# Low parts of feed-forward weights by an accumulating DMA in a two-layer hybrid decoder step on one Trainium2 core

## The chip, the cores and the metric

The program runs on one core of a Trainium2 chip. The metric is the device time of one execution in microseconds; the figure for a kernel is the median of its runs. The core has five engines with a queue of instructions each: TensorE (PE in the profile; PEld are its weight loads), VectorE (DVE), ScalarE (ACT), GpSimd (POOL) and SyncE (SP). DMAs are issued from the queues of ScalarE, SyncE and GpSimd and are carried out by 16 DMA engines.

## The reference

One inference step of a decoder of two layers, model width 1024, for 544 tokens: one prompt of 512 tokens and 8 decode streams of 4. All data is fp32.

```python
def _layer(x, pos0, st, p):
    x = x + 0.5 * _swiglu(_rmsnorm(x, p['norm_ffn1']), p['ffn1_in'], p['ffn1_out'])
    u = _rmsnorm(x, p['norm_mix']) @ p['w_in']
    ...                      # SSD, RWKV-7, S5 and pooling mixers, 256 columns each
    x = x + y @ p['w_out']
    x = x + 0.5 * _swiglu(_rmsnorm(x, p['norm_ffn2']), p['ffn2_in'], p['ffn2_out'])
def _swiglu(x, w_in, w_out):
    gate, up = jnp.split(x @ w_in, 2, axis=-1)
    return (jax.nn.silu(gate) * up) @ w_out        # inner width 2816
```

So there are four feed-forward layers, two around the mixers of each layer, and a final norm. The outputs are the normed activations and the new states of the mixers.

## The kernel before

**Products.** The activations lie feature-major on the chip, 8 tiles x of 128 rows by 544 tokens. Each fp32 operand of a product is split into a rounded part and a rest, both of type float32r: weights into whi and wlo, activations into xh and xl (hidden activations into hh and hl). A 128x128 block of weights takes three products for each half of the tokens (mm3, lines 807 to 815): whi with xh (line 813), whi with xl (814) and wlo with xh (815), that is 6 matmuls of 272 columns.

**Weights.** They are streamed once, in the order of use, as chunks of 8 blocks (CH=8), 512 KB each. fetch (lines 791 to 794) issues one DMA per chunk on ScalarE's queue into wraw, a buffer of its own kind with two copies. block (lines 795 to 806) works on half a chunk at a time (CB=4, 128x512): ScalarE casts it into whi (line 802), and an engine s.lo subtracts whi from the raw weights into wlo (line 803). s.lo is VectorE, but GpSimd during a part of the mixers. The pool wp holds three buffers each of whi and wlo. A raw buffer is free for the next fetch but one when both casts and both subtractions of its chunk have read it.

**A feed-forward layer** (ffn, lines 860 to 899). inph(m) forms one hidden tile: 8 blocks of gate and 8 of up, so two chunks. VectorE scales the gate by 1/rms (gt, line 878), ScalarE applies Silu (879), GpSimd multiplies by 1/rms (s, 880), VectorE multiplies by the up product (s, 881), ScalarE casts hh (883), GpSimd subtracts hl (884). outph(G) then adds a group of hidden tiles into the 8 tiles of x (893). The groups have 8, 8 and 6 hidden tiles, so a tile of x takes 8, 8 and 6 blocks. In the last group the norm of the next stage is prepared tile by tile: ScalarE squares (849), GpSimd sums (852). The first feed-forward layer also carries the making of the S5 tables (s5_prep) between its tiles, mainly on VectorE.

**Order.** Dependencies, semaphores and the order of each engine's queue are set by the Tile framework when the program is built, by a plan of its own and by the buffers that are free; the order of the lines is only its starting point. In the trace casts stand three half chunks ahead of TensorE's use.

Of the kernel before, what the change touches and what calls it, by code (L numbers as in the profile page):

```python
"""One inference step of the hybrid decoder: activations feature-major on chip, weights streamed once."""
# [6 lines left out]
def build_consts():  # L8
    c={}
    I=np.arange  # L10
    p=I(128)
# [8 lines left out]
    c['mak']=(same&(r[:,None]<r[None,:])).astype(np.float32)            # rows s, cols t  # L20
    c['min']=(r[:,None]<=I(64)[None,:]).astype(np.float32)
    c['mnoff']=(same&(r[None,:]<r[:,None])&(r[None,:]//16!=r[:,None]//16)).astype(np.float32)  # rows t, cols s
# [39 lines left out]
def colz(a): # [n*128] -> [128,n]  # L62
    return np.asarray(a).reshape(-1,128).T
# [14 lines left out]
def pack_mat(i,l):  # L78
    """[128, 2048]: w2 (2x128, rows 0-63), a2 (2x128, rows 64-127), g2 (256), pool (2x128, block diagonal) | glu (2 x 512)"""
    m=np.zeros((128,2048),np.float32)  # L80
    m[:64,0:256]=i['rwkv_w2'][l]; m[64:,256:512]=i['rwkv_a2'][l]; m[:,512:768]=i['rwkv_g2'][l]
    pw=i['pool_w'][l]
    for t in range(2):
        for g in range(2): m[g*64:g*64+64,768+t*128+g*64:768+t*128+g*64+64]=pw[t*2+g]
    gw=i['s5_glu_w'][l]
    m[:,1024:1536]=gw[:128]; m[:,1536:2048]=gw[128:]
    return m
# [7 lines left out]
def pack_s5h(i,l):  # L95
    re=i['state_s5_re'][l].transpose(2,1,0); im=i['state_s5_im'][l].transpose(2,1,0)  # n,g,b
    return np.ascontiguousarray(np.stack([np.concatenate([re,im],0),np.concatenate([im,re],0)]))
def merge(*flows):
    """interleaves generators by the time that they yield: flows are (start, pace, generator)"""
    q=[[t,i,f,g] for i,(t,f,g) in enumerate(flows)]  # L100
    while q:
        e=min(q,key=lambda e:(e[0],e[1]))
        try: e[0]+=e[2]*next(e[3])
        except StopIteration: q.remove(e)
class Mix:
# [14 lines left out]
    def mm544(s,lhsT,rhs,fn):  # L120
        """fn(psum [128,272], column slice) for the two halves of lhsT^T @ rhs [128,544]"""
        for i in range(2):
            ps=s.bank()[:,:H]; c=slice(i*H,(i+1)*H)
            s.nc.tensor.matmul(ps,lhsT,rhs[:,c],start=True,stop=True)
            fn(ps,c)
    def rsqrt(s,new,ss):
        """-2/sqrt of an SBUF tile, with one Newton step"""
# [7 lines left out]
    def rwkv_prep(s,U,fp,tp,R):  # L135
        """U: name -> flat tile [128,553] (called when needed). Decay-scaled operands of the chunked recurrence, into R."""
# [61 lines left out]
    def masked(s,E,t,src):  # L198
        """t [128,n,2,64] = src [128,n,64] in column block h for the rows of head h, zero elsewhere"""
# [5 lines left out]
    def rwkv_inv(s,R,hf,tp,qp):  # L205
        """for 4 chunks of 64: block-diagonal A operands and the transposed inverses of I - tril(A B^T)"""
# [19 lines left out]
        # triangular inverses of the 16x16 diagonal blocks: one block per lane  # L226
# [17 lines left out]
        # T = T16 + R T, R = T16 N off the diagonal blocks, R^4 = 0; the last step gives T^T  # L244
# [25 lines left out]
    def rwkv_quarter(s,R,q,tp,qp):  # L270
        """token-major and masked operands of 2 chunks x 2 pairs of heads"""
# [26 lines left out]
    def rwkv_chain(s,R,q,qp):  # L298
        """two chunks of the recurrence; R['ST'] is the state [(h,j), pair, (h,i)]"""
# [106 lines left out]
    # ------------------------------------------------------------------ SSD  # L406
    def conv(s,u,j,out,t):
        """causal convolution of 4 taps and silu: u flat [128,576] to out [128,544]; t scratch [128,572]"""
# [5 lines left out]
    def ssd_dt(s,dtr,fp,SD):  # L414
        """dtr [4,544]; step sizes, decays and their sums, token-major [128, 4 chunks + sample, 4 heads]"""
# [13 lines left out]
        # softplus(x) = max(x,0) + log1p(exp(-|x|)), log1p(e) = 2 artanh(e/(2+e))  # L429
# [16 lines left out]
        # cumulative sums in the chunk, totals  # L446
# [18 lines left out]
    def ssd(s,R,xs,BB,CCt,z,H0,state_out,emit,tp):  # L465
        """xs 2 x [128,544]; BB, CCt [128,2,544]; z(t): silu of the gate [128,544]. H0 DRAM [128 n,8 b,4 h,64 p]"""
# [6 lines left out]
        for c in (4,0,1,2,3):  # L473
# [3 lines left out]
            # broadcast cumulative sums  # L477
# [11 lines left out]
            # token major x*dt and B  # L489
# [51 lines left out]
        # gate, norm  # L541
# [13 lines left out]
    # ------------------------------------------------------------------ pool  # L555
    def pool(s,U,emit,tp):
        """U(t): flat [128,684]: 15 rows before | 512 | 8 x (15 + 4)"""
# [23 lines left out]
    # ------------------------------------------------------------------ S5  # L581
    S5OFF=dict(TP=0,GT=2048,CO=4096,COS=6144,SS=7168,RHO=8192,A4=9216,B4=9232,END=9248)
    def s5_prep(s,par,name,tp):
        """par DRAM [128,1072]: lam_re, lam_im, log_step [16 each], b_re, b_im, c_re, c_im [256 each]; rows (re|im, n).
        Fills a DRAM scratch [128, END] with the matrices and tables of the chunked recurrence (8 tokens to a chunk)."""
# [12 lines left out]
        def sincos(E,y,sn,cs,k):  # L598
            """y is reduced in place to [-pi,pi]"""
# [22 lines left out]
        # (a - 1)/lam  # L622
# [11 lines left out]
        # A1 = (pr | pi), A2 = (pi | pr) by row half  # L634
# [11 lines left out]
        # phases of a^8 and the modulus  # L646
# [5 lines left out]
        for g0 in range(0,16,4):  # L652
# [3 lines left out]
            # C a^d, d = 0..8  # L656
# [3 lines left out]
            # a^(7-s) b: transposed to (s,c') rows  # L660
# [7 lines left out]
            # Toeplitz blocks: K[c',(d,c)] behind 128 zeros, row s takes the window that starts 16 s earlier  # L668
# [16 lines left out]
    def s5(s,U,prep,glu,H0,state_out,emit,fp):  # L685
        """U(t): [128,8,80] (position in the chunk, prompt chunks | 8 sample at 0..3 | 8 sample at 4..7); H0 DRAM [2,128,16,8] (state, halves swapped)"""
# [4 lines left out]
        ud=s.dram.tile([2,8,16,8,80],F32,name="ud",bufs=2)  # t, g, c', s, k  # L691
        yd=s.dram.tile([2,8,16,8,72],F32,name="yd",bufs=2)  # t, g, c, t, k
# [8 lines left out]
        for t in range(2):  # L701
# [28 lines left out]
            HP=tl("HP",[8,96])  # state before each chunk: 0, h_1 .. h_63 | 8 sample | pad ; h_64 apart  # L730
# [40 lines left out]
# the flows of the mixers: start and pace in the merged order of emission  # L771
FL=dict(s5=(0,1),prep=(0,1.25),rwkv=(0,1.1),back=(29,0.9),smp=(11,0.417),ssd=(2,0.8),rest=(66,1.373))
# column order of w_in: tiles (name, first column, width)
WIN=[('wa',1796),('k0',1284),('s0',2052),('r0',1028),('s1',2180),('v0',1540),('gd',1924),('k1',1412),('p0',2308),('p1',2436),('v1',1668),('r1',1156),('B1',640),('B0',512),('C0',768),('dt',1024),('C1',896),('x0',256),('x1',384),('z1',128),('z0',0)]
# rows of w_out by mixer tile: y = ssd 0-1, rwkv 2-3, s5 4-5, pool 6-7
# [3 lines left out]
class Kern(Mix):  # L779
    def __init__(s,tc,nc,ctx,io):  # L780
        Mix.__init__(s,tc,nc,ctx)
        s.io=io
        s.psd=s.P("psd",2,space=bass.MemoryType.PSUM)
        s.wp=s.P("wp",3); s.xhl=s.P("xhl",1); s.hole=ExitStack()
        s.wi=0; s.lo=nc.vector
# [9 lines left out]
    def block(s):  # L795
# [3 lines left out]
        if j==0:  # L799
# [3 lines left out]
            s.lo.tensor_tensor(lo,raw,hi.bitcast(F32),op=OP.subtract)  # L803
# [12 lines left out]
    def mmdt(s,ps,st,cols):  # L816
        """4 columns of the weights, twice in their block: rows 0-3 take the high part, rows 4-7 the low one"""
# [6 lines left out]
    def split(s,k,x,scale=None,pool=False):  # L824
        """x (times a per-partition scale) as two float32r tiles that sum to it"""
# [27 lines left out]
    def rstd(s,acc,tp,mp=None,tag=None):  # L853
        """-2/rms of the columns"""
# [5 lines left out]
    def ffn(s,st,gnext,bg=iter(())):  # L860
        nc=s.nc
        with s.tc.tile_pool(name="ffh",bufs=12,reuse_waits="tile") as hp, s.tc.tile_pool(name="fft",bufs=2,reuse_waits="tile") as tp, s.tc.tile_pool(name="ffr",bufs=1,reuse_waits="tile") as rp:
# [32 lines left out]
            for gi,G in enumerate(GROUPS):  # L895
                for m in (G if gi==0 else G[1:]): inph(m); m>1 and next(bg,None)
                if gi<2: inph(GROUPS[gi+1][0])
                outph(G,gi==2)
        return nst
    def tail(s,po,hs,acc,tp):  # L900
        """last tile of the last FFN and the final norm, one half of the tokens after the other"""
# [27 lines left out]
    def mixers(s,l,st):  # L929
        nc=s.nc; io=s.io; V=nc.vector; G=nc.gpsimd; A=nc.scalar  # L930
        # the residual waits in DRAM
# [156 lines left out]
    def do_prep(s):  # L1088
        """tables of the S5 recurrences, in pieces between the tiles of an FFN"""
# [84 lines left out]
```

## Time and profile before

| | us |
|---|---|
| median of 2 runs | 2331.2 |
| runs | 2331.07 to 2331.32 |
| span of the profiled execution, first to last instruction | 2330.7 |
| TensorE busy in that span | 2249.1 |

The page gives the profiled execution by its span alone; the runs above lie 0.4 to 0.6 us over that span. All rows below are of that one execution. Engines are named by PE, DVE, ACT, POOL and SP, a q behind the name means the engine's queue (a DMA issue), and Lnnn is the line of the kernel. What stands behind an arrow in brackets released the instruction after an idle time.

### The profile page before, as it was taken

How to read it: one execution, taken by the hardware profiler on the slowest of the kernel's cores; microseconds unless marked ns; L12 is line 12 of the kernel's file. 1: busy time of each engine (PE TensorE's matmuls, PEld its weight loads, DVE VectorE, ACT ScalarE, POOL GpSimd, SP SyncE). 2: the span in 40 equal slices, each digit the busy share in tenths (PEclk: the TensorE clock that was granted, in tenths of full speed). 3: DMA queues.
4: the chain of work that ended last, by engine and by line, in shares of the span. 5: the costliest groups of instructions: out<-in, count | busy, mean ns of one | idle time of the engine just before them, and what ended most of it. 6: DMA issues, size and time to landing. Idle time of an engine off the chain costs nothing. (4 is left out here: it accounts for less than half of the span.)

```text
span 2330.7 us, 42034 instructions
## 1 busy us (share of the span) xinstructions
PE 2249.1 (97%) x17486; PEld 2195.2 (94%) x17486; DVE 1173.2 (50%) x2115; ACT 866.5 (37%) x1505; POOL 560.3 (24%) x570
## 2 busy tenths in 40 slices
PE   7999999989899999999999999999889999999997
PEld 7999999988789999999999999999878999999997
DVE  7937633466877533333443333343887673333334
ACT  5323323455445432222343232234554543223223
POOL 3312302433323220110222021125433222102012
PEclk9999999999999999999999999999999999999999
DMA  4433422533213222222222222235332132222222
GB/s 157 146 109 106 140 91 87 175 122 111 86 53 113 82 91 85 88 91 87 87 90 83 91 91 83 91 118 161 118 102 69 58 110 89 91 84 90 91 84 83
DMA packets 115407, 232.03 MB, mean 100 GB/s; under 512 B 33168, under 2 KB 57744, under 8 KB 115088
## 3 DMA queue, kind: packets, MB, share of 16 engines
q10 hardware_dynamic: 52208, 182.38, 22.7%
q1 hardware_dynamic: 63008, 46.95, 6.7%
q8 instruction: 138, 2.26, 0.4%
q14 instruction: 53, 0.43, 0.1%
HBM read 201.07 MB, written 28.22 MB: 98 GB/s over the span
## 5 line engine op out<-in xcount | busy, mean ns | idle before, releaser
L813 PE MATMUL pd<-xh,whi 128*128 128x272 f32 (+2 forms) x3712 | 1006.6, 290 | 18.0 <-ACT whi L802 9.7
L814 PE MATMUL pd<-xl,whi 128*128 128x272 f32 (+2 forms) x3712 | 1015.1, 290 | 4.1 <-DVE xl L831 4.0
L802 ACT CAST whi<-wraw 128x512 fp32r<-128x512 f32 x644 | 397.8, 619 | 1058.3 <-PE pd L814 979.9
L815 PE MATMUL pd<-xh,wlo 128*128 128x272 f32 (+2 forms) x3712 | 773.3, 289 | 3.4 <-DVE wlo L803 3.0
L813 PEld LDWEIGHTS pd<-xh,whi 128*128 128x128 f32 x3712 | 700.8, 189 | 24.3 <-ACT whi L802 11.4
L814 PEld LDWEIGHTS pd<-xl,whi 128*128 128x128 f32 x3712 | 704.7, 190 | 8.3 <-DVE xl L831 5.8
L803 DVE TENSOR_TENSOR wlo<-wraw,whi 128x512 fp32r<-128x512 f32 x544 | 393.1, 723 | 467.6 <-ACT whi L802 467.6
L815 PEld LDWEIGHTS pd<-xh,wlo 128*128 128x128 f32 x3712 | 590.6, 188 | 5.8 <-DVE wlo L803 3.6
L814 PE MATMUL pd<-hl,whi 128*128 128x272 f32 x1396 | 375.6, 288 | 0.0
L813 PE MATMUL pd<-hh,whi 128*128 128x272 f32 x1396 | 375.4, 287 | 0.0
L880 POOL TENSOR_TENSOR s<-gt,rsq_r 128x544 f32<-128x544 f32 x88 | 120.1, 1364 | 783.9 <-ACT gt L879 783.9
L815 PE MATMUL pd<-hh,wlo 128*128 128x272 f32 x1396 | 288.9, 288 | 0.0
L814 PEld LDWEIGHTS pd<-hl,whi 128*128 128x128 f32 x1396 | 263.1, 188 | 0.0
L813 PEld LDWEIGHTS pd<-hh,whi 128*128 128x128 f32 x1396 | 262.3, 188 | 0.0
L815 PEld LDWEIGHTS pd<-hh,wlo 128*128 128x128 f32 x1396 | 219.3, 188 | 0.0
L884 POOL TENSOR_TENSOR hl<-s,hh 128x544 fp32r<-128x544 f32 x88 | 122.7, 1395 | 385.4 <-ACT hh L883 385.4
L803 POOL TENSOR_TENSOR wlo<-wraw,whi 128x512 fp32r<-128x512 f32 x100 | 137.4, 1379 | 154.1 <-ACT whi L802 134.4
L893 DVE SCALAR_TENSOR_TENSOR x<-pd,x 128x544 f32<-128x544 f32 x95 | 68.8, 725 | 148.2 <-PE pd L815 148.2
L881 DVE TENSOR_TENSOR s<-pd,s 128x544 f32<-128x544 f32 x88 | 63.7, 723 | 148.8 <-PE pd L815 143.3
L878 DVE TENSOR_TENSOR gt<-pd,rsq_r 128x544 f32<-128x544 f32 x88 | 63.7, 724 | 137.0 <-PE pd L815 136.9
L883 ACT CAST hh<-s 128x544 fp32r<-128x544 f32 x88 | 57.0, 648 | 49.2 <-DVE s L881 49.2
L852 POOL TENSOR_TENSOR sqa<-sqa,sq 128x544 f32<-128x544 f32 x35 | 49.2, 1405 | 90.0 <-ACT sq L849 90.0
(471 smaller groups left out, 1953.0 us busy)
## 6 DMA issues: line engine op xcount, KB each, us to landing
wraw<-in_w ACTq DMA_DIRECT2D x322, 512.0 KB, 3.5
xd<-x SPq DMA_DIRECT2D x16, 272.0 KB, 3.3
x<-xd SPq DMA_DIRECT2D x16, 272.0 KB, 4.8
x<-in_x SPq DMA_DIRECT2D x8, 272.0 KB, 6.2
u<-yd SPq DMA_DIRECT2D x8, 272.0 KB, 3.1
s5d<-CA SPq DMA_DIRECT2D x8, 256.0 KB, 3.2
s5d<-GT SPq DMA_DIRECT2D x8, 256.0 KB, 2.8
s5d<-KZ SPq DMA_DIRECT2D x64, 32.0 KB, 1.7
```

The lines of the kernel that those rows point to most:

```text
L802: nc.scalar.copy(hi,raw)
L803: s.lo.tensor_tensor(lo,raw,hi.bitcast(F32),op=OP.subtract)
L813: nc.tensor.matmul(p,wh,rh[:,a:b],start=(n==0),stop=False)
L814: nc.tensor.matmul(p,wh,rl[:,a:b],start=False,stop=False)
L815: for p,a,b in o: nc.tensor.matmul(p,wl,rh[:,a:b],start=False,stop=(n==K-1))
L852: a=s.ntp.tile([128,T],F32,name="sqa",bufs=2); eng.tensor_tensor(a,st['acc'],sq,op=OP.add); st['acc']=a
L878: g=tp.tile([128,T],F32,name="gt"); nc.vector.tensor_tensor(v2(g),pg[:,:,:H],v2(r),op=OP.mult)
L880: s2=tp.tile([128,T],F32,name="s2"); nc.gpsimd.tensor_tensor(s2,g,r,op=OP.mult)
L881: nc.vector.tensor_tensor(v2(s2),pu[:,:,:H],v2(s2),op=OP.mult)
L883: nc.scalar.copy(hh,s2)
L884: nc.gpsimd.tensor_tensor(hl,s2,hh.bitcast(F32),op=OP.subtract)
L893: nc.vector.scalar_tensor_tensor(xv,po[:,:,:H],0.5,xv,op0=OP.mult,op1=OP.add)
```

## The change

The pool wp gets four buffers of whi and wlo in place of three. In the feed-forward layers, except in the last output group of each, the first half (i==0) of every chunk has its low part formed in another way: ScalarE writes the raw weights times -1 into wlo, rounded to that tile's type, and a DMA issued by GpSimd adds the raw weights to it. The second half keeps the subtraction. The mixers are left as they were but for the fourth buffer. The rest of the diff removes comments.

```diff
-        s.wp=s.P("wp",3); s.xhl=s.P("xhl",1); s.hole=ExitStack()
-        s.wi=0; s.lo=nc.vector
+        s.wp=s.P("wp",4); s.xhl=s.P("xhl",1); s.hole=ExitStack()
+        s.wi=0; s.lo=nc.vector; s.add=False
...
             nc.scalar.copy(hi,raw)
-            s.lo.tensor_tensor(lo,raw,hi.bitcast(F32),op=OP.subtract)
+            if s.add and i==0:
+                nc.scalar.mul(lo,raw,-1.0)
+                nc.gpsimd.dma_start(lo,raw,accum_op=OP.add)
+            else: s.lo.tensor_tensor(lo,raw,hi.bitcast(F32),op=OP.subtract)
             s.cur=(hi,lo)
...
     def ffn(s,st,gnext,bg=iter(())):
-        nc=s.nc
+        nc=s.nc; s.add=True
...
                 if gi<2: inph(GROUPS[gi+1][0])
+                s.add=gi<2
                 outph(G,gi==2)
```

## Rows read from the trace of the kernel before

**Rows 1.** The page's first part: busy time, share of the span, instructions, by engine

```profile
PE 2249.1 (97%) x17486; PEld 2195.2 (94%) x17486; DVE 1173.2 (50%) x2115; ACT 866.5 (37%) x1505; POOL 560.3 (24%) x570
```

**Rows 2.** 40 slices: us; busy PE, PEld, DVE, ACT, POOL; clock, DMA share, GB/s

```profile
0.00:58.30 58.30, 43.37 (x300) 41.16 (x301) 43.09 (x120) 31.55 (x49) 21.06 (x19) 0.97 0.43 156
...
233.10:291.30 58.20, 56.09 (x442) 54.30 (x441) 38.94 (x58) 21.29 (x38) 18.42 (x17) 1.00 0.47 141
...
990.50:1048.80 58.30, 58.30 (x467) 58.30 (x466) 19.63 (x30) 17.01 (x27) 10.87 (x8) 1.00 0.26 91
```

**Rows 3.** Timeline of ScalarE, feed-forward: start, us, what, [idle before, releaser]

```profile
1001.38 0.62 ACT L802 CAST whi<-wraw 128x512 fp32r<-128x512 f32 x1 [1.29 <-PE pd L814]
1002.76 0.33 ACTq L793 DMA_DIRECT2D wraw<-in_w  x1
1004.40 0.62 ACT L802 CAST whi<-wraw 128x512 fp32r<-128x512 f32 x1 [2.39 <-PE pd L814]
...
1007.41 0.62 ACT L802 CAST whi<-wraw 128x512 fp32r<-128x512 f32 x1 [1.35 <-PE pd L814]
1008.79 0.33 ACTq L793 DMA_DIRECT2D wraw<-in_w  x1
```

**Rows 4.** Timeline of VectorE in the same stretch

```profile
1002.03 0.69 DVE L803 TENSOR_TENSOR wlo<-wraw,whi 128x512 fp32r<-128x512 f32 x1 [2.02 <-ACT whi L802]
```

**Rows 5.** Timeline of ScalarE in the first 30 us

```profile
16.42 7.27 ACTq L793 DMA_DIRECT2D wraw<-in_w  x2
23.79 0.62 ACT L802 CAST whi<-wraw 128x512 fp32r<-128x512 f32 x1 [7.17 <-DVE wlo L803]
```

**Rows 6.** Waits of TensorE: total us, times, longest

```profile
PE pd L813 <- ACT whi L802: 9.7, 4, 7.4
...
PE pd L814 <- DVE xl L831: 4.0, 6, 1.1
...
PE pd L815 <- DVE wlo L803: 3.0, 3, 1.2
PE pd L813 <- DVE s L881: 2.9, 1, 2.9
```

**Rows 7.** Groups by line and shape: busy us, mean ns | idle before, releaser

```profile
L802 ACT CAST whi<-wraw 128x512 fp32r<-128x512 f32 x644 | 397.8, 619 | 1058.3 <-PE pd L814 979.9 <-DVE wlo L803 25.2 <-PE pd L815 12.8
L803 DVE TENSOR_TENSOR wlo<-wraw,whi 128x512 fp32r<-128x512 f32 x544 | 393.1, 723 | 467.6 <-ACT whi L802 467.6
...
L831 ACT ACTIVATE xh<-x,vec 128x544 fp32r<-128x544 f32 x48 | 34.9, 748 | 36.9 <-DVE x L893 25.1 <-DMA x<-in_x 4.7 <-POOL u_p L978 3.1
```

**Rows 8.** Timeline of GpSimd in the stretch of rows 3

```profile
1000.17 1.36 POOL L884 TENSOR_TENSOR hl<-s,hh 128x544 fp32r<-128x544 f32 x1 [4.73 <-ACT hh L883]
1006.14 1.36 POOL L880 TENSOR_TENSOR s<-gt,rsq_r 128x544 f32<-128x544 f32 x1 [4.61 <-ACT gt L879]
```

**Rows 9.** DMA issues: queue, count, KB each, median us from issue to landing

```profile
wraw<-in_w ACTq DMA_DIRECT2D x322, 512.0 KB, 3.5
...
h<-in_ssd SPq DMA_DIRECT2D x8, 256.0 KB, 2.9
...
rkd<-bo SPq DMA_DIRECT2D x4, 272.0 KB, 2.1
```

**Rows 10.** Line 793, the weight fetch: issue to landing

```profile
DMA to landing us min/median/max: 3.3/3.5/6.3
```

**Rows 11.** 5 us slices: us, TensorE busy (count), clock, DMA share, GB/s

```profile
10.00:15.00 5.00, 3.75 (x20) 1.00 0.99 379
15.00:20.00 5.00, 2.64 (x12) 0.83 0.49 172
```

**Rows 12.** Timeline of all engines around 52 us, first feed-forward layer

```profile
51.77 0.23 DVE L636 COPY A<-pr 64x144 f32<-64x144 f32 x1
...
52.35 1.37 POOL L880 TENSOR_TENSOR s<-gt,rsq_r 128x544 f32<-128x544 f32 x1 [6.79 <-ACT gt L879]
52.37 1.44 DVE L636 COPY A<-pi 64x144 f32<-64x144 f32 x1
```

## The prediction

> **What bounds the kernel now.** I read the page's busy line first: TensorE's matmuls cover 2249.1 of 2330.7 us, VectorE is busy half the span, ScalarE 37%, GpSimd 24% [rows 1]. So all of TensorE's idle time is 81.6 us, 3.5%. The table of slices says where: in a feed-forward slice such as 990.5 to 1048.8 us TensorE is busy for the whole slice and VectorE for a third of it, while the first slice alone lacks 14.9 us [rows 2]. The reader is to see that the engine that is relieved is not the one that is full.
>
> The cadence is in ScalarE's timeline: one cast of a half chunk (whi, four 128x128 blocks) every 3.01 us, each released by TensorE's last use of an older buffer [rows 3]. A chunk of eight blocks takes 6.03 us. After the second half's cast comes, on the same queue, the fetch of a later chunk (1002.76, 1008.79): it starts when VectorE has written that half's wlo (1002.03 + 0.69 = 1002.72), the last reader of the raw buffer [rows 3, 4]. ScalarE's queue is in order and a fetch that waits holds it: at 16.42 us two fetches took 7.27 us and the next cast came with 7.17 us of idle time behind VectorE's wlo [rows 5]. That is the row on which this prediction turns.
>
> The list of TensorE's waits is the ceiling of the gain: 3.0 us on VectorE's wlo, 4.0 on xl, 2.9 on s, and 9.7 on whi, of which 7.4 is the cold start [rows 6].
>
> **The change, part by part.** It applies to 60 half chunks of each feed-forward layer: 22 tiles of two chunks, and two output groups of eight chunks; the third group is excluded. Four layers make 240 of the 644 half chunks.
>
> VectorE loses 240 x 0.723 = 174 us of subtractions [rows 7]. TensorE does not wait for these in the steady stretch, so I cost that at nothing there; what hides it is TensorE's own full queue. In the first layer, where VectorE also forms the S5 tables, at most the waits on wlo, xl and s come back, 3.0 + 4.0 + 2.9 = 9.9 us [rows 6]; half of the subtractions go, and most of these waits are at the cold start, so I take 2 us.
>
> ScalarE gains 240 negating copies of 128x512. The cast of that size is 0.619 us, and the activation with a scale on 128x544 is 0.748, or 0.70 at 512 columns [rows 7]; I take 0.63, nearest to the cast, as the scale is a constant: 151 us more on an engine that is 37% busy. It holds up nothing by itself: between two casts it has 2.4 us of idle time [rows 3].
>
> GpSimd gains 240 DMA issues. An issue on ScalarE's queue takes 0.33 us [rows 3]; an ordinary GpSimd instruction of this size 1.36 us [rows 8]; I take about 0.8. With four buffers the first half of each chunk is cast at times like 1001.38 and 1007.41, so its negated copy ends some 1.27 us later, at 1002.65 and 1008.66. GpSimd's own s and hl run at 1000.17 and 1006.14 [rows 8] and are over by then. Behind the issue, which waits for the negated copy, stand only the next s or hl, and the issue is over by about 1003.5, 2.6 us before the next s.
>
> The new latency, call it D, runs from the end of the negated copy to the landing of the accumulating DMA (128x512 fp32, 256 KB, on chip to on chip). No row shows such a transfer or one issued by GpSimd. From below: a plain 272 KB store from the chip lands in 2.1 us. From above: if the load and the store back are done one after the other, 2.9 (a 256 KB load) + 2.1 = 5.0 us. It reads two operands, 512 KB, as the weight fetch does, which lands in 3.5 us, at most 6.3 [rows 9, 10]. I take that row, it is nearest in bytes, and 0.5 us for the slower issue: D = 4.0 us.
>
> By the Trainium skill, DMA: Bandwidth & Descriptors, section Anatomy of one DMA — SWDGE (gpsimd) path, a plain transfer from this queue costs 2.0 us plus its bytes over 436 GB/s, an estimate of 2.6 us for 256 KB; no row here shows it. By that figure the sum below would be the same.
>
> Three waits have to stand D. First, TensorE's use. With four buffers a cast begins three halves, 9.03 us, ahead of its use, and wlo is first read 0.5 us after that; less 1.27 us on ScalarE that leaves 8.2 us. Second, the raw buffer: cast, copy, D, then a fetch of 3.5 + 0.3 us must fit in two chunks, 12.05 us: D below 6.9. Third, and tightest, ScalarE's queue: if the fetch stands ahead of the next first-half cast, as the order before has it [rows 3], it must issue by 1007.41 - 0.33 = 1007.08, so D may be 1007.08 - 1002.65 = 4.4 us. With D = 4.0 the fetch could issue at 1006.65, 0.4 us inside that limit: hidden. If that cover goes, each 0.1 us over 4.4 costs 0.1 us per chunk, 24 us over the 240 chunks.
>
> The cold start has no lead. In place of the first subtraction, 0.72 us, stand the copy and D, 0.63 + 4.0, so the first wlo comes 3.9 us later, and 4.5 if the full DMA engines (share 0.99 in 10 to 15 us [rows 11]) stretch D. Against that TensorE idles 1.25 + 2.36 = 3.6 us of the time from 10 to 20 us [rows 11], partly for xl and wlo, and some of it goes as VectorE is freed. GpSimd's squares of x are delayed by two or three issues, and the first 1/rms with them. Bounds -1 and +6; I take +3.
>
> The fourth whi and wlo buffer also serves the mixers. There TensorE waits for the recurrences, hardly for whi (9.7 less the start's 7.4 leaves 2.3 us [rows 6]): between -2 and +2, I take 0. What may shift there is the order of instructions, worth a few us of either sign.
>
> Sum, against the profiled span: 2330.7 - 2 + 3 + 0 = 2331.7 us; the runs lie 0.4 to 0.6 us above the span, which makes 2332. I add 1 us for small collisions on GpSimd's queue where norm sums precede a layer: **2333 us**, 0.1% above the median of 2331.2.
>
> **The rivals.** *ScalarE held at the fetch (slower).* For it: the 7.17 us of rows 5, an order that already has the fetch ahead of the cast [rows 3], and a margin of only 0.4 us. Against it: a planner that thinks the DMA long would put the fetch behind the cast, where the bound is 6.9 us. It decides from D = 4.4 us; 2% is reached at D = 4.6 (0.2 x 240 = 48 us); at the upper bound D = 5.0 the price is 0.6 x 240 = 144, a time of 2477 us. It would show in the first-half casts, D + 1.6 us apart (copy and cast 1.27, issue 0.33) in place of 6.03.
>
> *Descriptors shut out by VectorE (a little slower).* A VectorE copy of 64x144 took 1.44 us when it ran beside GpSimd's s, where its neighbour of the same size took 0.23 [rows 12]: 1.2 us more, so the two hold each other up. While the S5 tables are made VectorE runs many copies and scalings; its busy time is still twice the steady one in the slice to 291 us [rows 2], and 291 / 6.03 = 48 chunks, of which I take 40. If GpSimd's issue waits for such work, D grows by about 1.0 us there, to 5.0, and 0.6 x 40 = 24 us are lost: 2357 us. The Trainium skill, SBUF — State Buffer, section Who interferes with whom, states this as a lock: GpSimd cannot write descriptors while VectorE runs a two-port copy. It also says that a subtraction of two tiles takes only the read side; by that rule the steady stretch, whose VectorE work is such operations, stays untouched. The trace agrees as far as that copy goes [rows 12]; it has no GpSimd DMA.
>
> *VectorE mattered more (faster).* If the freed time and the longer lead give back most of the 9.9 us of waits and a few us in the mixers, and the start costs nothing: 2324 us. For it: VectorE's long rows in the first layer; against it: TensorE's list of waits is short [rows 6]. A gain over 2% would need 47 of the 81.6 idle us, which nothing in the list offers.
>
> That the change does not do what it says would show as wlo subtractions on VectorE still near 544; nothing in the code suggests it.
>
> **How the numbers follow.** Forecast 0.45; ScalarE held 0.31; descriptors shut out 0.10; a few us faster 0.12; faster by over 2%, 0.02. The measurement tells about 2% of this kernel from no change, 47 us, so "same" holds the forecast, the 2357 and the 2324 case: 0.67; slower 0.31; faster 0.02. The range begins at 2318, below the faster case with its few us of reordering, and ends at 2477, where D is at its upper bound of 5.0; about 0.02 lies below and 0.16 above. The forecast's own range is 2326 to 2342.
>
> **What would show it.** VectorE's wlo count at 304 and its busy time near 1000 us; ScalarE's near 1015; GpSimd's DMA 240 times, 256 KB, with a landing near 3.5 to 4 us; casts in a feed-forward slice still 3.01 us apart and TensorE still full there; the first TensorE wait on wlo some 4 us long. The prediction is wrong if the casts come in pairs with more than 6.03 us per chunk, with ScalarE's idle time released by a DMA: then D is over 4.4 us and the fetch has held the queue.

## The result, and the profile after

The changed kernel takes 2361.99 us (median of 2 runs, 2359.84 to 2364.15) against 2331.2 before: 30.8 us or 1.3% longer, ratio 1.013 with a 95% interval of 1.010 to 1.016. The forecast was 2333 us, its range 2318 to 2477. That the two lie within 2% came as forecast and the time lies in the range, but the loss is 31 us where the sum gave 2.

First the page of the changed kernel: busy time, the DMA queue of the new transfers, the two new operations, the subtraction that is left, and the new DMA's landing. Line numbers have moved by 3: the cast is still L802, the negating copy is L804, the DMA L805, the subtraction L806, the matmuls L816 to L818.

```profile
PE 2252.7 (96%) x17486; PEld 2195.3 (93%) x17486; DVE 993.9 (42%) x1875; ACT 1000.2 (42%) x1750; POOL 765.1 (32%) x810
...
q0 software_dynamic: 34560, 62.93, 15.6%
...
L805 POOL DMA_DIRECT2D wlo<-wraw x240 | 209.1, 871 | 601.7 <-ACT wlo L804 586.2
...
L806 DVE TENSOR_TENSOR wlo<-wraw,whi 128x512 fp32r<-128x512 f32 x304 | 220.7, 726 | 63.5 <-ACT whi L802 63.0
...
L804 ACT ACTIVATE wlo<-wraw 128x512 fp32r<-128x512 f32 x240 | 150.6, 627 | 0.0
...
wlo<-wraw POOLq DMA_DIRECT2D x240, 256.0 KB, 3.3
```

Against [rows 1, 7], VectorE is relieved by 179 us, ScalarE carries 134 us more, and TensorE is busy for 2252.7 us, as before (2249.1). The 27.3 us that the span grew (2330.7 to 2358.0) are idle time of TensorE, but for the 3.6 us that it is busy for longer. The new DMAs are queue q0: 144 packets each (34560 / 240), 15.6% of the DMA engines' time.

The slices that answer to [rows 2], in the same columns:

```profile
0.00:58.30 58.30, 41.23 (x303) 40.32 (x304) 36.21 (x81) 33.38 (x53) 26.16 (x26) 1.00 0.62 183
233.10:291.30 58.20, 55.89 (x430) 53.83 (x429) 33.93 (x55) 25.94 (x48) 24.96 (x25) 0.97 0.72 185
990.50:1048.80 58.30, 58.30 (x466) 58.30 (x466) 13.23 (x20) 23.95 (x40) 21.38 (x19) 1.00 0.52 131
```

In the steady slice TensorE is as full as before, and VectorE goes from 19.63 to 13.23 us. So the loss is elsewhere. To find it I took the start of the same VectorE instruction in both traces (the gate of hidden tile 0, 3, 7, ..., the additions into x, the last addition of the mixers) and subtracted. The table gives how much each stage is longer than before, in one profiled execution of each kernel:

| stage | us in the kernel before | longer by |
|---|---|---|
| first feed-forward layer | 437.8 | 12.3 |
| mixers of layer 1 | 343.4 | -2.1 |
| second feed-forward layer | 398.0 | 0.3 |
| third, up to its fourth hidden tile | 43.7 | 3.0 |
| third, the rest | 355.3 | 0.0 |
| mixers of layer 2 | 338.7 | 13.6 |
| fourth feed-forward layer | 413.7 | 0.3 |

Three places carry the loss: the first layer, the entry of the third, and the second mixers, which the change was to leave alone but for the fourth buffer.

The timeline of ScalarE in the steady stretch, where the argument of the prediction turned:

```profile
1011.86 0.62 ACT L802 CAST whi<-wraw 128x512 fp32r<-128x512 f32 x1 [1.29 <-PE pd L817]
1012.39 0.63 ACT L804 ACTIVATE wlo<-wraw 128x512 fp32r<-128x512 f32 x1
1014.87 0.62 ACT L802 CAST whi<-wraw 128x512 fp32r<-128x512 f32 x1 [1.86 <-PE pd L817]
...
1016.70 0.33 ACTq L793 DMA_DIRECT2D wraw<-in_w  x1
1017.89 0.62 ACT L802 CAST whi<-wraw 128x512 fp32r<-128x512 f32 x1 [1.35 <-PE pd L817]
```

The negating copy ends at 1013.02 and the fetch, which waits for the landing, issues at 1016.70: D is 3.7 us (I had 4.0). The fetch is over at 1017.03 and the next first-half cast at 1017.89 is still released by TensorE: 0.86 us to spare, and casts 3.01 us apart.

TensorE's waits, to be read beside [rows 6]:

```profile
PE pd L818 <- DMA wlo<-wraw: 15.1, 6, 8.9
PE pd L816 <- ACT whi L802: 12.6, 4, 7.2
...
PE pd L818 <- DVE wlo L806: 4.5, 1, 4.5
```

Only six of 240 landings are waited for, and 8.9 of the 15.1 us are the very first. The 4.5 us is one wait for a subtraction on VectorE, the engine that has 240 fewer to do.

### The profile page after: what moved, and what is told of

Same layout as the page of the kernel before. It is cut to its first block, busy times and chain, and to the rows that moved or that the text cites. A ratio compares the mean times of both kernels' runs of the same rounds, so it can differ in the third digit from the quotient of the medians.

```text
span 2358.0 us, 42559 instructions
## 1 busy us (share of the span) xinstructions
PE 2252.7 (96%) x17486; PEld 2195.3 (93%) x17486; DVE 993.9 (42%) x1875; ACT 1000.2 (42%) x1750; POOL 765.1 (32%) x810
## 3 DMA queue, kind: packets, MB, share of 16 engines
q10 hardware_dynamic: 52208, 182.38, 23.5%
q0 software_dynamic: 34560, 62.93, 15.6%
## 4 chain that ended last, share of the span: by engine, by line
PE 82%; DVE 10%; DMA 3%; issue 2%; ACT 1%; POOL 1%; ACTq 0%; SPq 0%; DVEq 0%; POOLq 0%
PE pd L817 24%; PE pd L816 24%; PE pd L818 24%; PE pm L259 1%; PE pm L124 1%; DMA wlo<-wraw 1%; DMA s5d<-ph 1%; DVE u L411 1%; PE pm L292 1%; PE pm L758 1%; DVE TL L237 1%; DVE tmL L236 0%; PE pm L479 0%; PE pm L286 0%; DMA u<-yd 0%
## 5 line engine op out<-in xcount | busy, mean ns | idle before, releaser
L816 PE MATMUL pd<-xh,whi 128*128 128x272 f32 (+2 forms) x3712 | 1011.3, 291 | 27.9 <-ACT whi L802 12.6
L802 ACT CAST whi<-wraw 128x512 fp32r<-128x512 f32 x644 | 398.3, 620 | 948.6 <-PE pd L817 816.8
L818 PE MATMUL pd<-xh,wlo 128*128 128x272 f32 (+2 forms) x3712 | 775.3, 290 | 21.2 <-DMA wlo<-wraw 15.1
L816 PEld LDWEIGHTS pd<-xh,whi 128*128 128x128 f32 x3712 | 704.9, 190 | 35.7 <-ACT whi L802 19.6
L818 PEld LDWEIGHTS pd<-xh,wlo 128*128 128x128 f32 x3712 | 593.0, 189 | 25.6 <-DMA wlo<-wraw 16.6
L805 POOL DMA_DIRECT2D wlo<-wraw x240 | 209.1, 871 | 601.7 <-ACT wlo L804 586.2
L816 PE MATMUL pd<-hh,whi 128*128 128x272 f32 x1396 | 375.4, 287 | 0.0
L818 PE MATMUL pd<-hh,wlo 128*128 128x272 f32 x1396 | 288.9, 288 | 0.0
L816 PEld LDWEIGHTS pd<-hh,whi 128*128 128x128 f32 x1396 | 262.3, 188 | 0.0
L806 DVE TENSOR_TENSOR wlo<-wraw,whi 128x512 fp32r<-128x512 f32 x304 | 220.7, 726 | 63.5 <-ACT whi L802 63.0
L818 PEld LDWEIGHTS pd<-hh,wlo 128*128 128x128 f32 x1396 | 219.3, 188 | 0.0
L806 POOL TENSOR_TENSOR wlo<-wraw,whi 128x512 fp32r<-128x512 f32 x100 | 138.5, 1392 | 153.9 <-ACT whi L802 135.1
L804 ACT ACTIVATE wlo<-wraw 128x512 fp32r<-128x512 f32 x240 | 150.6, 627 | 0.0
```

The lines of the kernel that those rows point to most:

```text
L802: nc.scalar.copy(hi,raw)
L804: nc.scalar.mul(lo,raw,-1.0)
L805: nc.gpsimd.dma_start(lo,raw,accum_op=OP.add)
L806: else: s.lo.tensor_tensor(lo,raw,hi.bitcast(F32),op=OP.subtract)
L816: nc.tensor.matmul(p,wh,rh[:,a:b],start=(n==0),stop=False)
L818: for p,a,b in o: nc.tensor.matmul(p,wl,rh[:,a:b],start=False,stop=(n==K-1))
```

## The experiments

All times are compared with the kernel before, run beside them on the same chip (medians 2328 to 2331 us there). The kernels scatter more there than in the first measurement (before: 2323 to 2335 us), so a difference of 3 us in one profile is read only where it repeats. The letters of the theories are those of each expectation.

**1. The fourth buffer without the DMA** (all low parts by the subtraction, four buffers everywhere).

```diff
-            if s.add and i==0:
+            if False:
```

> Edit: four whi and wlo buffers, all subtractions back on VectorE. Theory A (most of the loss outside the first feed-forward layer is the fourth buffer: it alters the planned order of the mixers): the mixers of the second layer lose about 14 us as in the changed kernel, those of the first gain about 2 and the layer after them loses 3, the first feed-forward layer loses nothing; in all 2331 + 15 = 2346 us. Rival B (all of the loss is the DMA, by late wlo and by the fetch that waits on ScalarE's queue): 2331 us, the mixers' stages within 2 us of before.

Measured: 2341.55 us, ratio 1.0051 (1.0031 to 1.0072), some 12 us over before. In its profile, which is of the slowest of its six runs, the first layer is 2.7 us shorter and the second mixers 20.7 us longer, every feed-forward layer behind the first unchanged. So the second mixers lose by the buffer alone, with no DMA in the program, as theory A has it. The second mixers before, in the changed kernel and here: us from the start, length, busy time of TensorE, granted clock, DMA share, GB/s:

```profile
1578.20:1916.90 338.70, 315.16 (x2352) 0.97 0.33 103
1591.70:1944.00 352.30, 317.84 (x2354) 0.96 0.32 100
1574.30:1933.70 359.40, 324.89 (x2354) 0.94 0.32 97
```

TensorE idles for 23.5 us there before and for 34.5 us in both kernels with the fourth buffer: 11 us that repeat. The rest, in which the two differ, is longer busy time at a lower granted clock. In the instruction streams TensorE's order in the mixers is the same as in the changed kernel and another one than before. The waits of TensorE there agree too: 4.0 us on whi (once) and, on tiles of the mixers, 5.0 and 5.6 on vu, 2.5 on xs in both kernels; before it was 0.5 on whi, 2.9 on vu.

**2. The DMA with three buffers.**

```diff
-        s.wp=s.P("wp",4)
+        s.wp=s.P("wp",3)
```

> Edit: the changed kernel with three buffers of whi and wlo instead of four. A: the mixers keep the order and the length of before; the first feed-forward layer loses 10 to 20 us (the lead of wlo is one half chunk, 3.0 us, shorter); the other three feed-forward layers lose nothing, as D = 3.6 us still fits in the 5.2 us that three buffers leave; in all 2341 to 2351 us. B: as A in the first layer, but also late in the other layers, above 2362 us.

Measured: 2365.81 us, ratio 1.0156 (1.0137 to 1.0174). The second mixers are 2.2 us shorter than before: their loss is gone, as the theory has it. But the first layer loses 16.4 us, and each later feed-forward layer 6 to 10, nearly all by the end of its first output group. Theory A had no such cost and asked for 2351 us at most; B's figure, above 2362 us, came out. Run 4 has the cause.

**3. The DMA from the second feed-forward layer on, four buffers.**

```diff
-            if s.add and i==0:
+            if s.add and i==0 and s.wi>=528:
```

> Edit: the changed kernel with the accumulating DMA only from the second feed-forward layer on (180 in place of 240), four buffers kept. A: the 12 us of the first layer come back, the mixers stay as slow as in the changed kernel: 2350 us, like the fourth buffer alone. B: the loss goes with the count of DMAs, 180/240 of 31 us: 2354 us, and there would be late wlo in the other layers.

Measured: 2343.11 us, ratio 1.0058 (1.0035 to 1.0080). The first layer is 5.7 us shorter than before, the second mixers 19.8 longer; the 180 DMAs that are left cost 3.0 us, all at the entry of the third feed-forward layer. That is the pattern of theory A, some 7 us below its total.

**4. The same with three buffers.**

```diff
-        s.wp=s.P("wp",4)
+        s.wp=s.P("wp",3)
...
-            if s.add and i==0:
+            if s.add and i==0 and s.wi>=528:
```

> Edit: three buffers and the accumulating DMA only from the second feed-forward layer on; 180 subtractions of 128x512 leave VectorE. A: no change from before, 2331 us within 3, TensorE full in the feed-forward slices, mixers as before. B: the DMA costs something wherever it stands: above 2340 us. A third view, that VectorE's freed time is worth something after all: below 2328 us.

Measured: 2348.77 us, ratio 1.0083 (1.0065 to 1.0101). B's figure, above 2340 us, came out, and A's 2331 us did not. TensorE's and VectorE's orders are those of the kernel before throughout, but for the 180 subtractions that are gone, so the loss is not an altered order of these two, and still each of the three layers loses 6 us. The timeline of ScalarE in the second feed-forward layer:

```profile
875.04 0.33 ACTq L793 DMA_DIRECT2D wraw<-in_w  x1
875.47 0.62 ACT L802 CAST whi<-wraw 128x512 fp32r<-128x512 f32 x1 [3.58 <-DVE gt L881]
876.00 0.65 ACT L882 ACTIVATE gt<-gt 128x544 f32<-128x544 f32 x1
876.56 0.61 ACT L804 ACTIVATE wlo<-wraw 128x512 fp32r<-128x512 f32 x1
...
881.42 0.33 ACTq L793 DMA_DIRECT2D wraw<-in_w  x1
```

and of GpSimd:

```profile
876.74 1.36 POOL L883 TENSOR_TENSOR s<-gt,rsq_r 128x544 f32<-128x544 f32 x1 [4.16 <-ACT gt L882]
878.06 0.86 POOL L805 DMA_DIRECT2D wlo<-wraw  x1
```

The fetches are 6.38 us apart, and the DMA's issue at 878.06 plus its usual 3.3 us to the landing is 881.4, the time of the second fetch. That is a ring: fetch, cast, Silu, negating copy, GpSimd's s ahead of the DMA's issue, landing, and only then the next fetch, with everything behind it on ScalarE held. This is the rival "ScalarE held at the fetch", 0.35 us over the 6.03 of TensorE per chunk, as long as s or hl stands ahead of the issue. Once they don't (the output group from 905 us on, fetches 5.2 to 5.6 us apart), the ring is shorter than TensorE's chunk, the lead builds up, and nothing more is lost.

**5. The landing made later, by one and by three GpSimd additions** (on the changed kernel; they write a scratch tile; range(3) in the second).

```diff
                 nc.scalar.mul(lo,raw,-1.0)
+                fill=s.wp.tile([128,128],F32,name="fill",bufs=1)
+                for q in range(1): nc.gpsimd.tensor_tensor(fill,lo[:,q%4,:].bitcast(F32),lo[:,(q+1)%4,:].bitcast(F32),op=OP.add)
                 nc.gpsimd.dma_start(lo,raw,accum_op=OP.add)
```

> The changed kernel with one GpSimd addition of 128x128 (about 0.4 us by the 0.61 us that a 128x256 one takes in the first layer) between the negating copy and the DMA issue of every affected half chunk, so that the low part lands about 0.4 us later. Theory A (the fetch on ScalarE's queue waits for the landing, and the cast behind it has 0.86 us of slack in the steady layers): still hidden there, 0 to +4 us against the changed kernel, so about 30 us over the kernel before. Rival B (every microsecond on GpSimd's queue or of landing time costs): 240 x 0.4 = 96 us over the changed kernel. Rival C (the limit is the four buffers, 8 us away): also nothing; it parts from A in the next run.

> The same with three such additions, about 1.2 us more until the landing. Theory A: 1.2 - 0.86 = 0.3 us over the slack, per chunk, in some 200 chunks whose fetch stands ahead of the next first-half cast: +60 us against the changed kernel (between 30 and 110, as the 0.4 us is not measured for this size), casts about 6.4 us apart per chunk in place of 6.03, ScalarE's idle time ahead of the fetch released by the DMA. Rival B: 240 x 1.2 = +290 us. Rival C (four buffers or the raw buffer are the limit): within 10 us of the changed kernel, casts 6.03 us apart per chunk.

Measured: 2365.21 us (ratio 1.0145, 1.0130 to 1.0159) with one, 2659.73 us (1.1409, 1.1391 to 1.1428) with three. One addition costs nothing that can be told against the changed kernel (2361.99 us); three cost 294.5 us more than one. The timeline of ScalarE with three:

```profile
1009.79 0.33 ACTq L793 DMA_DIRECT2D wraw<-in_w  x1
1010.22 0.62 ACT L802 CAST whi<-wraw 128x512 fp32r<-128x512 f32 x1 [5.71 <-DMA wlo<-wraw]
1010.75 0.62 ACT L804 ACTIVATE wlo<-wraw 128x512 fp32r<-128x512 f32 x1
1011.27 0.60 ACT L802 CAST whi<-wraw 128x512 fp32r<-128x512 f32 x1
1017.12 0.33 ACTq L793 DMA_DIRECT2D wraw<-in_w  x1
```

Fetch to fetch is 7.33 us: the casts come in a pair, then ScalarE stands 5.7 us until the DMA lands. D is 1017.12 - 1011.37 = 5.75 us, and the rule of the prediction, D + 1.6 us per chunk, gives 7.35. The surplus, 7.33 - 6.03 = 1.30 us, makes the 294.5 us if 227 of the 240 chunks pay it. With one addition the copy ended at 1018.59 and the fetch issued at 1022.84: D = 4.25, still under the 4.4 us of the prediction, and the next cast was released by TensorE. So the limit lies between 4.25 and 5.75 us where it was placed at 4.4, and beyond it the price is as worked out. Theory A was right here and my figure for it (+60 us) was wrong: I had an addition at 0.4 us, while three of them and the step to the issue put the issue 2.4 us behind the copy, where it was 0.30 without them:

```profile
1011.46 1.99 POOL L806 TENSOR_TENSOR fill<-wlo 128x128 f32<-128x128 f32 x3 [4.21 <-ACT wlo L804]
1013.75 0.87 POOL L807 DMA_DIRECT2D wlo<-wraw  x1 [0.30 <-POOL fill L806]
```

Rival B met the second figure (+290) and is refuted by the first run, where it asked for 96 us.

**6. Three additions, and the fetch on SyncE's queue.**

```diff
-        s.fetched=s.nc.scalar.dma_start(t,s.io['w'][c]).ins
+        s.fetched=s.nc.sync.dma_start(t,s.io['w'][c]).ins
```

> The kernel with three GpSimd additions ahead of each DMA, 295 us slower than the one with a single addition, but the weight fetch is issued from SyncE's queue in place of ScalarE's. The landing still comes 5.7 us after the negating copy. Theory A (what costs is that the waiting fetch holds the casts behind it on ScalarE): the next limit is the raw buffer, 6.9 us, so the three later feed-forward layers run at 6.03 us per chunk again and their share of the loss, some 80 us each, goes; in the first layer and the mixers SyncE's own transfers now wait behind fetches, so I give the total a wide 2350 to 2420 us. Rival G (the later landing itself costs, through the raw buffer or TensorE's use): the chunks stay at 7.3 us, about 2660 us.

Measured: 2399.39 us, ratio 1.0307 (1.0290 to 1.0325), 260 us less than with the fetch on ScalarE. ScalarE's timeline:

```profile
1042.08 0.62 ACT L802 CAST whi<-wraw 128x512 fp32r<-128x512 f32 x1 [1.39 <-PE pd L819]
1042.60 0.63 ACT L804 ACTIVATE wlo<-wraw 128x512 fp32r<-128x512 f32 x1
...
1048.10 0.62 ACT L802 CAST whi<-wraw 128x512 fp32r<-128x512 f32 x1 [1.33 <-PE pd L819]
```

and SyncE's:

```profile
1048.50 0.33 SPq L793 DMA_DIRECT2D wraw<-in_w  x1
```

The landing is as late as the fetch shows, 1048.50 - 1043.23 = 5.3 us behind the copy, well over 4.4, and the chunk is back at 6.02 us. From their fourth hidden tile on the second, third and fourth feed-forward layers lose nothing at all. What holds up is thus not the landing itself but a fetch that waits for it on the queue which also carries the casts. Of the 70 us that are left 64 lie in the first layer (29) and the two mixers (16 and 19). The changed kernel loses 12 of these in the first layer and 14 in the second mixers too, without the additions; for the rest, SyncE carries the transfers of the S5 tables and the mixers there, and which of the waits costs most is open.

**7. The first two chunks of the program without the DMA** (two of the 240 are left out, four buffers).

```diff
-            if s.add and i==0:
+            if s.add and i==0 and s.wi>=16:
```

> The changed kernel, but the first two chunks of the program keep the subtraction on VectorE. Theory A (the cold start is one part of the first layer's 12 us, the stalls at 60 to 65 and 121 to 123 us are the larger one, from low parts that come late while ScalarE, GpSimd and VectorE make the S5 tables): 2 to 5 us below the changed kernel, some 26 us over the kernel before. Rival D (the whole loss of the first layer follows from the late start): all 12 us go, some 18 us over the kernel before.

Measured: 2350.32 us, ratio 1.0079 (1.0066 to 1.0093), 12 us less than the changed kernel has by its ratio. The first layer's loss falls from 12.3 to 2.2 us. Theory A, which gave the cold start 2 to 5 us, fell; rival D, that the whole loss follows from the late start, has the right total. The two traces show how the two versions part. In the changed kernel's timeline TensorE waits 8.87 us for the first low part, and there is a second stall at 60.7 us:

```profile
17.48 0.82 PE L818 MATMUL pd<-xh,wlo 128*128 128x272 f32 x2 [8.87 <-DMA wlo<-wraw]
...
65.22 0.82 PE L818 MATMUL pd<-xh,wlo 128*128 128x272 f32 x2 [4.50 <-DVE wlo L806]
```

The first comes from GpSimd's queue, where the DMA's issue stands behind squares of x, and then lands after 7.1 us among the first loads:

```profile
7.72 2.63 POOL L844 TENSOR_TENSOR q<-x 128x544 f32<-128x544 f32 x2 [1.10 <-DMA x<-in_x]
10.29 1.02 POOL L805 DMA_DIRECT2D wlo<-wraw  x1
```

By the first gate (31.3 us against 29.2) only 2.1 us of that are left. The second stall is an order. VectorE of the changed kernel around it:

```profile
50.02 0.69 DVE L806 TENSOR_TENSOR wlo<-wraw,whi 128x512 fp32r<-128x512 f32 x1 [0.32 <-issue]
...
64.48 1.28 DVE L806 TENSOR_TENSOR wlo<-wraw,whi 128x512 fp32r<-128x512 f32 x2
```

and with the first two chunks spared:

```profile
52.70 0.68 DVE L806 TENSOR_TENSOR wlo<-wraw,whi 128x512 fp32r<-128x512 f32 x1
...
63.97 0.68 DVE L806 TENSOR_TENSOR wlo<-wraw,whi 128x512 fp32r<-128x512 f32 x1
```

In the first, no subtraction is done between 50.71 and 64.48 us: some seventy short instructions, nearly all for the S5 tables, stand ahead of the two that are due, one of them for a cast that ended at 56.25. In the second, one is put in at 52.70. The planned order of VectorE changes with the first two chunks, and the wait of 4.5 us goes with it. Whether a late start alone, with the order kept, would have cost the same was not tried.

Against the kernel before, the account is another. TensorE's lag in us behind the kernel before, by the start of the same matmul into pd, counted from the first:

| matmul into pd | us in the kernel before | changed kernel | two chunks spared | fourth buffer, no DMA (run 1) |
|---|---|---|---|---|
| 289th | 54.2 | 2.1 | 0.9 | 1.8 |
| 341st | 65.4 | 4.4 | -3.7 | 0.7 |
| 769th | 125.5 | 12.4 | 2.6 | 0.7 |

The kernel before has a stall of its own between the first two, which the spared version is free of:

```profile
57.75 0.36 PE L813 MATMUL pd<-xh,whi 128*128 128x272 f32 x1 [2.86 <-DVE s L881]
```

So the stall at 60.7 us puts the changed kernel only 2.3 us further back. The larger part, 8.0 of 12.3 us, comes behind it, while the S5 tables are made, which is the place that theory A named. The spared version loses 6.3 us there as well, and ends near the kernel before because it had gained 4.7 us at the stall. This repeats: between the last two of these matmuls the eight kernels with the DMA in the first layer lose 5.2 to 11.0 us, the five without it 0.0. One of the changed kernel's waits there, and GpSimd ahead of it:

```profile
123.30 0.82 PE L818 MATMUL pd<-xh,wlo 128*128 128x272 f32 x2 [2.16 <-DMA wlo<-wraw]
...
118.73 0.74 POOL L594 TENSOR_TENSOR ph<-ph,er 128x256 f32<-128x256 f32 x1
119.42 0.89 POOL L805 DMA_DIRECT2D wlo<-wraw  x1
```

The negating copy had ended at 117.89, so the issue stood 1.5 us behind GpSimd's rows for the tables, and the landing then took 3.8 us. How the 8 us divide between such queues and the transfers themselves (median landing 3.9 us from 65 to 126 us) is open.

**8. Four buffers only where the DMA is used, three in the last output groups and the mixers.**

```diff
-        s.wp=s.P("wp",4)
+        s.wp=s.P("wp",1)
...
-            hi=s.wp.tile([128,CB,128],F32R,name="whi"); lo=s.wp.tile([128,CB,128],F32R,name="wlo")
+            r=s.ring=(s.ring+1)%(4 if s.add else 3)
+            hi=s.wp.tile([128,CB,128],F32R,name=f"whi{r}",bufs=1); lo=s.wp.tile([128,CB,128],F32R,name=f"wlo{r}",bufs=1)
```

> The changed kernel with four buffers of whi and wlo only in the groups that use the DMA, and three in the last output groups and the mixers, as before. Theory A (the mixers of the second layer lose 14 to 20 us because the fourth buffer alters the planned order there): that part goes back to within 5 us of the kernel before, the whole is 10 to 17 us over it. Rival E (the mixers lose because the feed-forward layers hand them another state, whatever the buffers): still about 30 us over it. The planned order in the mixers is near that of the kernel before, but not the same, so a few us of either sign may be left.

Measured: 2348.71 us, ratio 1.0067 (1.0049 to 1.0085), some 16 us over before: theory A, and not E. The second mixers are 3.3 us longer than before in place of 13.6. Over all profiles the split is plain: the second mixers are 10 to 21 us longer in the seven kernels with four buffers there, and between -2 and +4 in the six with three, with and without the DMA. The late start is untouched here (12.2 us).

**9. Both remedies, and the same buffers with no DMA.**

> Both remedies together: three buffers in the last output groups and the mixers, four elsewhere, and the first two chunks of the program without the DMA; 238 DMAs are left. If the two losses are separate (late start 10 to 12 us, mixers of the second layer some 11 us), both go: 5 to 12 us over the kernel before. If they are one (the later start sets the planner's order in the mixers), the second remedy adds nothing to the first: 17 to 20 us over it, as the run with the three buffers alone.

> The same buffers as in the run before, and no DMA at all: every low part by the subtraction. TensorE's planned order in the mixers is the same as there, so the difference of the two is the price of the 238 DMAs with their negating copies and of the relief of VectorE. Theory A (hidden in the steady layers, a few us where a layer starts): 2 to 8 us faster than the run before, -2 to +4 us against the kernel before. Rival F (VectorE's relief is worth something once the order is held fixed): slower than the run before.

Measured: 2342.17 us with the 238 DMAs (ratio 1.0064, 1.0047 to 1.0082), 2326.01 us with none (1.0000, 0.9985 to 1.0014). The first lies between what the two cases of its expectation asked for, so it does not settle whether the losses add: in its profile the first layer's loss is gone (0.9 us), but its ratio is hardly below that of run 8. The pair gives the price of the DMA itself. TensorE's order is the same in both throughout, so 16 us (15 by the ratios) is what the DMAs cost with the buffers held fixed, twice my upper figure; by the profiles 3.9 us lie in the first layer, 5.7 at the entry of the third and 5.6 in the second mixers. Rival F, a gain from VectorE's relief, falls. The 5.6 us are not shown to be the DMA's, as the mixers hold none. The second mixers with the DMAs and without, in the columns of run 1:

```profile
1581.60:1924.30 342.70, 319.99 (x2353) 0.96 0.35 104
1572.80:1909.90 337.10, 315.19 (x2352) 0.97 0.34 105
```

TensorE idles there for nearly as long in both (22.7 and 21.9 us) and is busy for 4.8 us longer at a lower granted clock, in one profile each of kernels whose runs spread over 14 and 17 us.

The entry of the third layer is the fetch again. ScalarE of the changed kernel:

```profile
1198.17 0.33 ACTq L793 DMA_DIRECT2D wraw<-in_w  x1
1198.54 1.28 ACT L130 ACT_TABLE_LOAD   x1 [2.48 <-DMA wlo<-wraw]
1199.83 0.66 ACT L130 ACTIVATE rsq_r<-ms 128x544 f32<-128x544 f32 x1
```

1/rms of the layer's norm stands behind a fetch that waits for a landing. The first gate needs it, and TensorE then waits 1.9 us for the gate (3.4 and 3.6 us in runs 9 and 8, 0.4 us for a cast before and without the DMA).

**10. Four buffers in the first feed-forward layer alone, no DMA.**

> No DMA, and the fourth buffer only in the first feed-forward layer, the one stage in which it gained (2.7 us with it alone, 5.7 us where the DMA began later); three buffers everywhere else, as before. If that gain stands by itself: 2 to 6 us faster than the kernel before, the first version to beat both. If a slight change of order in the mixers takes it back: -2 to +5 us.

Measured: 2326.74 us, ratio 0.9997 (0.9984 to 1.0009). The first layer is 4.2 us shorter, the second mixers 2.7 us longer; no gain that can be told. No version here beats the kernel before.

## Why the prediction was right or wrong

*What bounds the kernel, and that VectorE's relief buys nothing: right.* 179 us fewer on VectorE, and TensorE as full as before in every steady stretch. The kernel without the DMA is the faster one at equal buffers (run 9).

*The new operations: right.* The negating copy takes 0.627 us (0.63), the issue 0.87 (about 0.8), D is 3.7 us (4.0), the landing 3.3 us against the 3.5 of the row that I chose.

*The third wait, ScalarE's queue at the fetch, limit 4.4 us: right in place and price.* Its size lies in the bracket that the runs leave, 4.25 to 5.75 us. The changed kernel is on the good side by 0.7 to 0.86 us; runs 4, 5 and 6 show the rival on the other side. I gave it 0.31; with D at 3.7 it did not decide in the steady stretch. What I missed is that the limit holds only where the lead is built up and nothing stands ahead of DMA or fetch: it is passed with three buffers and s ahead of the issue, and for a chunk or two at a layer's entry. "1 us for small collisions on GpSimd's queue where norm sums precede a layer" should have been 3 us for 1/rms behind the held fetch.

*The cold start, +3 with bounds -1 and +6, and -2 for VectorE's long rows: failed.* The first wait on wlo, which I put at some 4 us, is 8.87: the issue stands behind the squares and the landing takes 7.1 us. At the first gate the loss is still 2.1 us, in the bounds. I took that for the end of it. The late start meets a planned order that interleaves the S5 tables with the layer, and the order that came out leaves VectorE's remaining subtraction behind them, 2.3 us worse than the stall of the kernel before. I had counted only on fewer subtractions making waits go; a subtraction that is left can stand later. The largest part, 8.0 of the 12.3 us, comes from 65 to 126 us, where the DMAs and the tables share GpSimd's and ScalarE's queues. The sum has no term for that. Ten of the 12.3 us go with two of the 240 DMAs, but 6.3 of the 8.0 stay; what goes is the stall.

*The fourth buffer in the mixers, "between -2 and +2, I take 0 ... worth a few us of either sign": failed, the largest term.* It is +13.6 in the changed kernel's profile, 11 of them idle time of TensorE, and by ratio some 12 us for the buffer alone. My row (2.3 us of waits for whi) bounds what a longer lead can give, and says nothing of what another order costs in a stage bound by chains of small instructions. That the new order is what costs, and not the buffer in another way, is argued and not shown: the orders of runs 8 to 10 in the second mixers also differ from the one before, and lose 4 us at most. Which instruction costs the most is open.

*The rivals.* "Descriptors shut out by VectorE" named 2357 us, near the result, by luck: its place, the stretch where the S5 tables are made, loses 8 us, but not in its way, and the rest of the loss lies elsewhere. From 25 to 160 us:

```profile
L805 POOL DMA_DIRECT2D wlo<-wraw x19: 803/881/903, 29.0 to 154.5; - x19
...
DMA to landing us min/median/max: 3.3/3.5/6.3
```

The issue takes 0.80 to 0.90 us there, as in the steady stretch (0.85 to 0.89), and the median landing is 0.2 us later, not 1.0. The Trainium skill, SBUF — State Buffer, section Who interferes with whom, states that GpSimd cannot write descriptors while VectorE runs a two-port copy; no issue in this stretch is lengthened by it. "VectorE mattered more" is refuted by run 9.

*The range.* That the time lies in 2318 to 2477 us says little for the sum: the upper part of the range stands for the held fetch at D = 5.0, and the forecast's own range ended at 2342. The terms that made the loss, the first layer and the second mixers, were taken at +1 and 0.

## What to carry to other kernels

When an operation is replaced by a DMA, look first for what waits for the landing on an in-order queue, and what else stands on that queue: 1.35 us over the slack cost nearly 300 us here, and another queue for the waiting fetch took 260 back. A stage whose slack is built up can hide a latency that the first chunks, a layer's entry and a smaller number of buffers cannot, so price those places one by one. And where a planner sets the order, a buffer more is a change to every stage that uses the pool: measure it alone before counting it at nothing.

## What the runs showed of the hardware that was not expected

The accumulating DMA of 256 KB, from on-chip memory to on-chip memory, lands in 3.3 us (3.2 to 7.1), about as fast as a 512 KB fetch (3.5), and its issue holds GpSimd for 0.87 us. The Trainium skill, DMA: Bandwidth & Descriptors, section Anatomy of one DMA — SWDGE (gpsimd) path, gives a plain transfer of that size an estimate of 2.6 us; the accumulating one is 0.7 us above it.

GpSimd's 128x128 addition took 0.46 us by itself (run 5, one addition). Three of them took 1.53 us where VectorE ran nothing beside them (from 1043.31, run 6), and 1.99 us with a subtraction beside them (run 5, from 1011.46; the subtraction ran from 1011.91 to 1012.60). So GpSimd was held up by some 0.46 us; the subtraction was not, with 0.69 us against 0.68 in run 6.

After the stall at 60.7 us TensorE came back at 0.43 us per matmul in place of 0.29; in that 5 us slice the granted clock was 0.66, so it stood at the lower of its two levels, 1.2 GHz, for the larger part of it:

```profile
65.00:70.00 5.00, 4.78 (x26) 4.79 (x27) 4.21 (x11) 1.28 (x1) 0.00 (x0) 0.66 0.96 266
```

That is 26 matmuls against 42 in a full slice at 1.00. Less the 0.22 us in which TensorE still waited, the stall of 4.5 us cost some 1.7 us more behind it. The kernel before shows the same after its wait of 2.86 us at 57.75: 32 matmuls from 60 to 65 us, at 0.73.
